# A hybrid decoder layer: every 512-column group projected in a pair, seven products for eight in 21 more chunks

## The chip, the cores and the metric

The kernel runs on one core of a Trainium2 chip. The metric is device time in microseconds (us) of one launch. Engines: TensorE (PE, matmuls), VectorE (DVE), ScalarE (ACT), GpSimd (POOL), SyncE (SP, issues DMAs).

## The reference

One layer on 256 tokens of 4096 features, in float32, cut to what matters:

```
h = rms_norm(x, norm_w)
proj = h @ w_in                        # 4096 x 13328 columns
rq, rk, rv, rg, mq, mk, mv, mg, sz, sxbc, sdt, lx, lg = split(proj)
y_ret  = rms_norm(retention(rq, rk, rv), ret_gn_w) * silu(rg)     # 4 heads of 256
y_moba = moba_attention(mq, mk, mv)    * silu(mg)                 # 8 heads of 128
y_ssm  = rms_norm(ssd(conv(sxbc), sdt) * silu(sz), ssm_norm_w)    # 16 heads of 64
y_lru  = rg_lru(conv(lx))              * silu(lg)                 # 8 blocks of 128
x = x + concat(y_ret, y_moba, y_ssm, y_lru) @ w_out               # 4096 x 4096
return rms_norm(x, final_norm_w)
```

Nearly all of the arithmetic lies in the two projections, `h @ w_in` and `y @ w_out`.

## The kernel before

**A product in float32.** Both operands are split in two halves of a rounded float32 type: the high one is a cast (ACT, L189, `whi`), the low one the rest (DVE, L190, `wlo`). A product is three matmuls, high by high, low by high, high by low, which add up in one bank of PSUM (`products`, L742 to 744, in single groups; `three`, L806 to 808, in pairs).

**Groups, chunks, half chunks.** The columns of `w_in` come in 25 groups: the first (rv, 1040 columns), then 24 of 512 columns in the order ret (4), bc (2), xs (2), mv (2), moba (4), lx (2) and the gates sz, rg, mg, lg (2 each). The 4096 rows are 16 chunks `c` of two tiles of 128 rows. Weights of a chunk of a group (512 KB) are loaded by SP in `raw` (5 buffers) and split two steps ahead of their use. Groups 0 to 16 run one by one, in the loop around L748. The last four pairs of groups run in `pair_in`: the pair has four accumulators `q` (two token halves, two groups), and a step is half a chunk, the weights of one group of the pair.

**Fast chunks.** In the chunks that `FAST_IN` names, `seven` multiplies the 2 x 2 blocks (tokens by weights of a pair) with seven products for eight, 21 matmuls for 24. Weights of the second step are combined with those of the first by four subtractions on DVE (L202, 203, 205, 207) and split in tiles `thi` and `tlo`; tokens are combined by `mix_of` in tiles `ys` ahead of time. Four more accumulators `r` take sums that belong to several outputs. They are added to the results behind the last fast chunk by `side` operations (`add`), two for each step. The output projection (`pair`, 4 pairs of 512 columns) does the same with `FAST`.

**Branch work.** What follows a projection (rotation, scores, convolution, scan, normalisation, gates) is cut in units in the queue `todo`; `slot()` takes one for each step. In a pair, units run until the first fast chunk, since the four `r` banks are those that the units use. Where instructions stand in the end is decided by a scheduler, engine by engine.

**Scaling by token.** The input is not normalised ahead of the projection: results are scaled by `rstd` when they leave PSUM (`rows_of`). Late groups use x tiles multiplied by a power of two per token (`rescale`, L277, tile `pwr`), and then `rres`.

**The end.** `row` adds x to the projected row, squares it on ACT for the norm, and multiplies by the final norm's weights into `rs`; `store_rows` scales `rs` (L945) and writes it out. x (`xres`) and these weights (`fw`) are loaded from POOL, six loads for each pair.

Of the kernel before, what the change touches and what calls it, by code (L numbers as in the profile page):

```python
# [18 lines left out]
P = 128  # L19
# [80 lines left out]
def tile_kernel(ctx: ExitStack, tc: tile.TileContext, t: dict):  # L100
# [74 lines left out]
    def split(n):  # L175
        if n >= len(chunks):
            return
        where, _, kt, nk, w = chunks[n]
        if where == "x":
            split_x(xraws.pop(n))  # L180
        raw = raws.pop(n)
        if where == "hold":
            hi, lo = pair_of(mixed[-1][0], "t", mixed[-1][1], 1024)
        else:
            hi, lo = pair_of(wp, "w", SPL + 1, WW)
        parts[n] = hi, lo

        def high_low(h, l, raw, a, b):
            A.copy(h[:, a:b], raw[:, a:b])  # L189
            V.tensor_tensor(l[:, a:b], raw[:, a:b], h[:, a:b].bitcast(F32), ALU.subtract)  # L190

        cuts = FIRST if n == 0 else CUTS if n == 1 else ((512, 1024),) if where == "fastb" else ((0, nk * w),)
        for a, b in cuts:
            high_low(hi, lo, raw, a, b)
        if where == "fasta":
            raws["a"] = raw
        elif where == "fastb":

            ra, rb = raws.pop("a"), raw
            (ha, la), (hb, lb) = (pair_of(mixed[-1][0], "t", mixed[-1][1], 1024) for _ in range(2))  # L200
# [61 lines left out]
    def stat_done():  # L262
        A.copy(ones_r, ones)
        m = sp.tile([P, 2], F32, name="m2", bufs=1)
        V.reduce_sum(m, xss, axis=AX.X)
# [20 lines left out]

    yT = [yp.tile([P, 2, S], F32, name=f"y{i}") for i in range(16)]

# [7 lines left out]
    def t1(name="t1"):  # L296
        return sp.tile([P, 512], F32, name="t1", bufs=5)

    lent = itertools.cycle([12, 14])

    def rows_of(ps, func=AF.Copy, lend=False):

        if lend:

            i = next(lent)
            tk = [yT[i + k].rearrange("p a b -> p (a b)") for k in range(2)]
        else:
# [118 lines left out]
    def moba_scores(h, q, k):  # L426
# [4 lines left out]
        V.scalar_tensor_tensor(s[:, 0:384], negd, 2.0 ** -(h + 1) / MS, ps[:, 0:384], op0=ALU.mult, op1=ALU.add)  # L431
        m = sp.tile([P, 4], F32, name="mm")
        V.reduce_max(m[:, 0:1], s[:, 0:128], axis=AX.X)
# [118 lines left out]
    def lru_split(n):  # L552
        w = st.pop(("lw", n))
        wh, wl = (sp.tile([P, 2, P], F32R, name=x) for x in ("lwh", "lwl"))
        A.copy(wh, w)
# [52 lines left out]

    def after(what, ps):
        name, i = what  # L610
        if name == "rv":
            st["v"] = [br.tile([P, 1024], F32, name="v") for _ in range(2)]
# [11 lines left out]
        elif name == "mv":  # L624
            if i == 0:
                st["v"] = [br.tile([P, 1024], F32, name="v") for _ in range(2)]
            for k in range(2):
                A.activation(st["v"][k][:, i * 512:(i + 1) * 512], ps[k], AF.Copy, scale=rstd[:, k:k + 1])
        elif name == "ret":
            tk = rows_of(ps, lend=True)  # L630
            qk = br.tile([P, 4, S], F32, name="qk")
# [5 lines left out]
        elif name == "bc":  # L637
            tk = rows_of(ps, lend=True)
            o = b4()
# [14 lines left out]
        elif name == "xs":  # L654
            tk = rows_of(ps, lend=True)

# [19 lines left out]
        elif name == "moba":  # L676
            tk = rows_of(ps, lend=True)
            qk = br.tile([P, 4, S], F32, name="qk")
# [5 lines left out]
        elif name == "lx":  # L684
            tk = rows_of(ps)

# [15 lines left out]
        else:  # L702
            todo.extend(gate(rows_of(ps, AF.Silu), Y_GATE[name] + 4 * i))
            if name == "sz" and i == 1:
# [79 lines left out]

    def mix_of(xs, c):
        pool = mixed[-1][0]
        q = pool.tile([P, 512], F32, name="ma")
# [3 lines left out]
        s = pool.tile([P, 512], F32, name="mb")  # L791
        s1, s2, s3, s4 = (s[:, i * P:(i + 1) * P] for i in range(4))
# [3 lines left out]
        V.tensor_tensor(s4, a12, s2, ALU.subtract)  # L796
        hl = pool.tile([P, 1024], F32R, name=f"ys{c}")
        A.copy(hl[:, 0:512], s)
# [42 lines left out]
    def pair_in(j, g, n):  # L841
# [10 lines left out]
        for c in range(NCH):  # L852
            for i in range(2):
# [8 lines left out]
                if c in fast:  # L862
                    if r is None:
                        assert not todo
                        r = [other[0].tile([P, 512], F32, name=other[1]) for _ in range(4)]
                    seven(xT, c, i, q, r, p, tt, c == fast[0], c == fast[-1])
                    if i == 1 and c == fast[-1]:

                        rows = [gp.tile([P, 1024], F32, name="ge") for _ in range(2)]
                        e11, e21, e12, e22 = (rows[k // 2][:, k % 2 * 512:(k % 2 + 1) * 512] for k in range(4))  # L870
                        side.append(lambda: A.copy(e11, r[0]))
# [7 lines left out]
                if r is None:  # L879
                    slot()  # L880
            if what == "sz":
                rescale(KC * c)
                rescale(KC * c + 1)
            if what == "rg":
                if c == 5:
                    while todo:
                        slot()
                    br_stack.close()
                    mixed.append((mx_stack.enter_context(tc.tile_pool(name="mx", bufs=1)), 3))
                    mixed[-1][0].tile([P, 48], F32, name="gap")  # L890
                if c in MIX_IN:
# [9 lines left out]
        else:  # L901
            for e, k in ((e11, 0), (e12, 1), (e21, 2), (e22, 3)):
                V.tensor_tensor(e, e, q[k], ALU.add)
                A.activation(e, e, AF.Silu, scale=rres[:, k // 2:k // 2 + 1])
            for i in range(2):
                todo.extend(gate([rows[i][:, 0:512], rows[i][:, 512:1024]], Y_GATE[what] + 4 * i))
        return n
# [17 lines left out]
    rs = [fp.tile([P, D], F32, name=f"rs{k}") for k in range(2)]  # L925
    mixed.append((ctx.enter_context(tc.tile_pool(name="mp", bufs=1)), 4))
# [21 lines left out]
    def extra(o):  # L948
# [3 lines left out]
        for k in range(2):  # L952
            xt = fp.tile([P, 512], F32, name="xres", bufs=4)
            nc.gpsimd.dma_start(out=xt, in_=t["x"][k * P:(k + 1) * P, o * 512:(o + 1) * 512])
            xres.append(xt)
        return fw, xres

    def pair(o, n, q, r, spare):
# [10 lines left out]
        def early():  # L969

            u = mixed[-1][0].tile([P, 512], F32, name="ma")
            w = mixed[-1][0].tile([P, 512], F32, name="mb")
            side.append(lambda: A.copy(u, p1))
# [11 lines left out]
        for c in range(NCH):  # L985
            if o == 0 and 1 <= c <= len(MIX):
                mix_of(yhl, MIX[c - 1])
            for i in range(2):
# [10 lines left out]
                else:  # L999
# [3 lines left out]
                    else:  # L1003
                        mms(yhl, q[2 + i], 1, c, p, c == 0, c == (LATE - 2 if end and i else NCH - 1))
                if c == fast[-1] and i == 1:
# [25 lines left out]

    MIX = (7, 9, 12, 2, 4)
    for j, o in enumerate(FAST):
# [52 lines left out]
```

## Time and profile before

| | us |
|---|---|
| median of three runs | 1551.89 (1551.76 to 1551.99) |
| the profiled execution | 1552.94 |
| its span, first to last instruction | 1551.2 |
| PE busy | 1534.5 |
| DVE busy | 1054.2 |
| ACT busy | 804.1 |
| POOL busy | 30.0 |

Terms of a sum come from the profiled execution, so they are taken from its own time. An engine is busy while an instruction of it runs; matmuls overlap, so PE is busy throughout even if its instructions are long.

### The profile page before, as it was taken

What the parts mean: (1) busy time and instruction counts of PE and PEld (TensorE: products, weight loads), DVE (VectorE), ACT (ScalarE), POOL (GpSimd) and SP (SyncE); (2) the same over time, 40 slices, a digit from 0 to 9 for tenths busy, and PEclk for the clock granted to TensorE, in tenths of its full rate; (3) what the DMA queues carried; (4) which work ended last, traced back from release to release, by engine and by line L of the source; (5) the groups of instructions that cost most, each with busy time, mean ns of one, the idle gap of its engine ahead of it and who ended that gap; (6) DMA issues with size and microseconds to landing.
All of it is one profiled execution on the core that took longest, in us unless ns stands there. A gap on an engine that the chain in (4) does not pass through costs nothing.

```text
span 1551.2 us, 19411 instructions
## 1 busy us (share of the span) xinstructions
PE 1534.5 (99%) x7166; PEld 1279.7 (83%) x7166; DVE 1054.2 (68%) x1431; ACT 804.1 (52%) x1077; POOL 30.0 (2%) x58
## 2 busy tenths in 40 slices
PE   9999999999999999999999999999999999999996
PEld 8988888888888788888888888888888888888885
DVE  5564444475565644545557876989879888887978
ACT  5644444454455434444448746555556555554553
POOL 0000000000000100000000000000000000000000
PEclk9999999999999999999999999999999999999998
DMA  8975555555555555545464555565655667575764
GB/s 310 310 239 189 174 174 184 181 191 191 196 187 181 202 191 192 175 174 179 169 209 170 186 191 177 166 215 202 206 189 207 214 212 237 190 238 208 238 221 165
DMA packets 89215, 311.34 MB, mean 201 GB/s; under 512 B 10352, under 2 KB 12032, under 8 KB 89120
## 3 DMA queue, kind: packets, MB, share of 16 engines
q1 hardware_dynamic: 83808, 296.70, 55.1%
q0 software_dynamic: 3440, 10.65, 2.4%
q10 hardware_dynamic: 1872, 2.76, 0.5%
q8 instruction: 56, 0.92, 0.2%
q14 instruction: 39, 0.32, 0.1%
HBM read 305.84 MB, written 4.22 MB: 200 GB/s over the span
## 4 chain that ended last, share of the span: by engine, by line
PE 92%; DMA 3%; DVE 3%; ACT 1%; issue 1%; POOL 0%; SPq 0%; ACTq 0%; POOLq 0%; DVEq 0%
PE pm L744 15%; PE pm L742 15%; PE pm L743 15%; PE pm L808 7%; PE pm L807 7%; PE pm L806 7%; PE pb L807 7%; PE pb L806 7%; PE pb L808 7%; DMA b<-in_x 1%; DVE wlo L190 1%; PE pb L319 1%; DMA b<-in_xt 1%; ACT whi L189 1%; DMA b<-csd 0%
## 5 line engine op out<-in xcount | busy, mean ns | idle before, releaser
L190 DVE TENSOR_TENSOR wlo<-raw,whi 128x1024 fp32r<-128x1024 f32 (+3 forms) x545 | 642.1, 1185 | 433.6 <-ACT whi L189 412.5
L189 ACT CAST whi<-raw 128x1024 fp32r<-128x1024 f32 (+3 forms) x545 | 552.5, 1019 | 584.0 <-PE pm L743 332.0
L742 PE MATMUL pm<-whi,xT 128*128 128x512 f32 (+1 forms) x1152 | 445.9, 387 | 1.9 <-ACT whi L189 0.9
L744 PE MATMUL pm<-wlo,xT 128*128 128x512 f32 (+1 forms) x1152 | 443.1, 385 | 1.5 <-DVE wlo L190 1.4
L743 PE MATMUL pm<-whi,xT 128*128 128x512 f32 (+1 forms) x1152 | 442.3, 384 | 0.0
L744 PEld LDWEIGHTS pm<-wlo,xT 128*128 128x128 f32 x1152 | 216.4, 188 | 46.0 <-DVE wlo L190 3.3
L742 PEld LDWEIGHTS pm<-whi,xT 128*128 128x128 f32 x1152 | 216.6, 188 | 45.0 <-ACT whi L189 1.6
L743 PEld LDWEIGHTS pm<-whi,xT 128*128 128x128 f32 x1152 | 216.6, 188 | 41.8
L806 PE MATMUL pm<-whi,xT 128*128 128x512 f32 (+1 forms) x438 | 170.1, 388 | 0.0
L808 PE MATMUL pm<-wlo,xT 128*128 128x512 f32 (+1 forms) x438 | 169.9, 388 | 0.1
L807 PE MATMUL pm<-whi,xT 128*128 128x512 f32 (+1 forms) x438 | 169.7, 387 | 0.0
L806 PE MATMUL pb<-whi,xT 128*128 128x512 f32 x398 | 155.3, 390 | 0.0
L807 PE MATMUL pb<-whi,xT 128*128 128x512 f32 x398 | 155.0, 389 | 0.0
L808 PE MATMUL pb<-wlo,xT 128*128 128x512 f32 x398 | 155.0, 389 | 0.0
L189 ACT CAST thi<-raw 128x512 fp32r<-128x512 f32 (+1 forms) x123 | 75.1, 629 | 60.0 <-DVE raw L202 36.1
L808 PEld LDWEIGHTS pm<-wlo,xT 128*128 128x128 f32 x438 | 82.3, 188 | 17.3 <-DVE wlo L190 0.6
L807 PEld LDWEIGHTS pm<-whi,xT 128*128 128x128 f32 x438 | 82.3, 188 | 16.6
L806 PEld LDWEIGHTS pm<-whi,xT 128*128 128x128 f32 x438 | 82.3, 188 | 16.5
L808 PEld LDWEIGHTS pb<-wlo,xT 128*128 128x128 f32 x398 | 74.7, 188 | 15.6
L807 PEld LDWEIGHTS pb<-whi,xT 128*128 128x128 f32 x398 | 74.7, 188 | 15.5
L806 PEld LDWEIGHTS pb<-whi,xT 128*128 128x128 f32 x398 | 74.7, 188 | 15.5
L190 DVE TENSOR_TENSOR tlo<-raw,thi 128x512 fp32r<-128x512 f32 (+1 forms) x123 | 84.4, 698 | 1.1 <-ACT thi L189 0.8
(277 smaller groups left out, 1156.5 us busy)
## 6 DMA issues: line engine op xcount, KB each, us to landing
raw<-in_w SPq DMA_DIRECT2D x384, 512.0 KB, 3.5
raw<-in_wo SPq DMA_DIRECT2D x128, 512.0 KB, 5.4
raw<-in_w SPq DMA_DIRECT2D x31, 520.0 KB, 5.0
b<-in_x SPq DMA_DIRECT2D x8, 512.0 KB, 6.1
xres<-in_x POOLq DMA_DIRECT2D x16, 256.0 KB, 5.7
b<-in_xt SPq DMA_DIRECT2D x15, 257.0 KB, 4.9
fw<-in_fnw POOLq DMA_DIRECT2D x8, 256.0 KB, 6.2
out<-rs ACTq DMA_DIRECT2D x8, 256.0 KB, 2.9
```

What stands on the lines that cost most here:

```text
L189: A.copy(h[:, a:b], raw[:, a:b])
L190: V.tensor_tensor(l[:, a:b], raw[:, a:b], h[:, a:b].bitcast(F32), ALU.subtract)
L319: T.transpose(ps[:, e * S + k * P:e * S + (k + 1) * P], tk[k][:, (2 * u + e) * P:(2 * u + e + 1) * P], ident)
L742: T.matmul(ps[:, :w], xh, hi[:, o:o + w], start=first, stop=False)
L743: T.matmul(ps[:, :w], xl, hi[:, o:o + w], start=False, stop=False)
L744: T.matmul(ps[:, :w], xh, lo[:, o:o + w], start=False, stop=last)
L806: T.matmul(ps, x[0], hi, start=first, stop=False)
L807: T.matmul(ps, x[1], hi, start=False, stop=False)
L808: T.matmul(ps, x[0], lo, start=False, stop=last)
```

## The change

1. All 24 groups of 512 columns run in pairs through `pair_in`; only rv is left to the old loop.
2. Pairs ret (second), bc, xs, moba (both) and lx have fast chunks 10, 12 and 14: 18 more. In the output projection they are 4, 6, 6 and 5 for 3, 5, 5 and 5: 3 more.
3. The scaling of the x tiles by token moves to the first pair, chunks 4 to 15, and to the first chunks of the second. From the second pair on, results are scaled by `rres`.
4. The mixed x tiles of chunks 10, 12 and 14 are made in chunks 5 to 7 of the second pair.
5. Split weight sums of the early pairs lie in tiles `yb` or `b4`, one set of four; behind the last fast chunk results are built in y tiles 12 to 15 (or `qk`).
6. In the output projection x is loaded straight into `rs`, and `row` multiplies in place. There are no `xres` buffers to wait for, so all x loads are queued at its start.
7. Small tiles get a pool of their own, and the split LRU weights one tile.

The core of the diff:

```diff
-NP = 17
-FAST_IN = {17: (), 19: (11, 13), 21: (3, 5, 7, 9, 11, 13), 23: (5, 9, 11, 13)}
-FAST = {0: (7, 9, 12), 2: (2, 4, 7, 9, 12), 4: (2, 4, 7, 9, 12), 6: (2, 4, 7, 9, 12)}
+EARLY = (10, 12, 14)
+FAST_IN = {1: (), 3: EARLY, 5: EARLY, 7: EARLY, 9: (), 11: EARLY, 13: EARLY, 15: EARLY, 17: (),
+           19: (11, 13), 21: (3, 5, 7, 9, 11, 13), 23: (5, 9, 11, 13)}
+FAST = {0: (6, 8, 10, 12), 2: (2, 4, 6, 8, 10, 12), 4: (2, 4, 6, 8, 10, 12), 6: (2, 4, 6, 8, 10)}
...
-    for gi, (what, cols) in enumerate(GROUPS[:NP]):
+    for gi, (what, cols) in enumerate(GROUPS[:1]):
...
+    def t_tiles():
+        if not mixed:
+            n = len(banks)
+            pool, tag = (yp, "yb") if n <= 5 else (br, "b4")
+            a, b, c, d = (pool.tile([P, 1024], F32R, name=tag, bufs=4) for _ in range(4))
+            return (a, b), (c, d)
+        return [pair_of(mixed[-1], "t", 3 if len(mixed) == 1 else 4, 1024) for _ in range(2)]
...
-            if what == "sz":
-                rescale(KC * c)
-                rescale(KC * c + 1)
+            if g == 1 and c >= 4:
+                rescale(KC * c - 8)
+                rescale(KC * c - 7)
+            if g == 3:
+                if c < 4:
+                    rescale(24 + KC * c)
+                    rescale(25 + KC * c)
+                elif 5 <= c < 8:
+                    k = c - 5
+                    at = gp.tile([P, 1024], F32R, name="ge") if k < 2 else sp.tile([P, 1024], F32R, name="s3", bufs=1)
+                    mix_of(xT, EARLY[k], at)
...
-        V.tensor_tensor(rs[k][:, o * 512 + a:o * 512 + b], xres[:, a:b], fw[:, a:b], ALU.mult)
+        V.tensor_tensor(xres[:, a:b], xres[:, a:b], fw[:, a:b], ALU.mult)
...
-            xt = fp.tile([P, 512], F32, name="xres", bufs=4)
+            xt = rs[k][:, o * 512:(o + 1) * 512]
```

**Where the order moves.** The first place is the bc pair, behind retention's norm. On DVE, in before, the norm's second reciprocal (of a tile `t`) and the products with it stand among low parts of weights:

```order
L190 TENSOR_TENSOR wlo<-raw,whi 128x1024 x2
L378 RECIPROCAL t_2719<-t_2719 128x512
L190 TENSOR_TENSOR wlo<-raw,whi 128x1024
L395 SCALAR_TENSOR_TENSOR y_106<-y_106,par,t_2719 128x256 x2
L395 SCALAR_TENSOR_TENSOR y_107<-y_107,par,t_2719 128x256 x2
L190 TENSOR_TENSOR wlo<-raw,whi 128x1024 x5
```

On DVE, in the changed kernel, at the same place (`raw<-raw` is a weight sum, `yb` holds the sums' halves):

```order
L194 TENSOR_TENSOR wlo<-raw,whi 128x1024 x2
L399 RECIPROCAL t_2942<-t_2942 128x512
L194 TENSOR_TENSOR wlo<-raw,whi 128x512
L416 SCALAR_TENSOR_TENSOR y_110<-y_110,par,t_2942 128x256 x2
L416 SCALAR_TENSOR_TENSOR y_111<-y_111,par,t_2942 128x256 x2
L206 TENSOR_TENSOR raw<-raw 128x512
L194 TENSOR_TENSOR wlo<-raw,whi 128x1024
L207 TENSOR_TENSOR raw<-raw 128x512
L194 TENSOR_TENSOR yb<-raw,yb 128x512
L209 TENSOR_TENSOR raw<-raw 128x512
L194 TENSOR_TENSOR yb<-raw,yb 128x512
L211 TENSOR_TENSOR raw<-raw 128x512
```

The weight sums of the first fast chunk now follow the norm directly. On PE, in before, the norm's second pair of matmuls (`ones_r`) stands in a plain row of products:

```order
L744 MATMUL pm<-wlo,xT 128x512
L375 MATMUL pb<-r_2694,ones_r 128x512
L375 MATMUL pb<-r_2695,ones_r 128x512
L742 MATMUL pm<-whi,xT 128x512
L743 MATMUL pm<-whi,xT 128x512
```

On PE, in the changed kernel, 24 matmuls behind that norm, where the second half of fast chunk 10 begins (`ge` and `yb` are the mixed tokens and the weight sums):

```order
L828 MATMUL pm<-wlo,ge 128x512
L826 MATMUL pm<-whi,xT 128x512
L827 MATMUL pm<-whi,xT 128x512
L826 MATMUL pb<-whi,xT 128x512
L827 MATMUL pb<-whi,xT 128x512
L826 MATMUL pb<-yb,ge 128x512
L827 MATMUL pb<-yb,ge 128x512
L828 MATMUL pm<-wlo,xT 128x512
```

Matmuls of the following chunk (`whi,xT`, `wlo,xT`) stand between the mixed product and those with `yb`, and among them. The second place is POOL at the start of the output projection. In before, the loads of two pairs:

```order
L950 DMA fw<-in_fnw 128x512
L954 DMA xres<-in_x 128x512 x2
L950 DMA fw<-in_fnw 128x512
L954 DMA xres<-in_x 128x512 x3
L950 DMA fw<-in_fnw 128x512
```

In the changed kernel, there:

```order
L989 DMA fw<-in_fnw 128x512
L993 DMA rs_10052<-in_x 128x512
L993 DMA rs_10053<-in_x 128x512
L989 DMA fw<-in_fnw 128x512
L993 DMA rs_10052<-in_x 128x512
L993 DMA rs_10053<-in_x 128x512
```

Twelve more loads of x into the two `rs` tiles follow, and only then the next `fw`, which waits for a buffer.

## Rows read from the trace of the kernel before

**Rows 1.** The page, busy time, share of the span and instructions of each engine.

```profile
PE 1534.5 (99%) x7166; PEld 1279.7 (83%) x7166; DVE 1054.2 (68%) x1431; ACT 804.1 (52%) x1077; POOL 30.0 (2%) x58
```

**Rows 2.** The page, chain that ended last, share of the span by engine.

```profile
PE 92%; DMA 3%; DVE 3%; ACT 1%; issue 1%; POOL 0%; SPq 0%; ACTq 0%; POOLq 0%; DVEq 0%
```

**Rows 3.** Waits of PE: line waited for, us in total, times, longest us.

```profile
PE pm L744 <- DVE wlo L190: 1.4, 2, 1.0
```

**Rows 4.** Timeline of PE, pair mg: start us, us, instruction.

```profile
1108.35 0.39 PE L806 MATMUL pm<-whi,xT 128*128 128x512 f32 x1
...
1113.79 0.39 PE L806 MATMUL pm<-whi,xT 128*128 128x512 f32 x1
```

**Rows 5.** Windows: length; PE, PEld, DVE, ACT, POOL busy; PE clock, DMA share, GB/s.

```profile
99.00:192.80 93.80, 93.12 (x422) 77.07 (x423) 49.40 (x79) 39.96 (x48) 0.52 (x1) 1.00 0.56 196
286.60:380.40 93.80, 93.80 (x426) 77.86 (x426) 57.01 (x66) 48.43 (x60) 1.06 (x2) 1.00 0.55 186
1060.00:1070.00 10.00, 10.00 (x46) 8.29 (x45) 9.44 (x13) 5.73 (x9) 0.00 (x0) 1.00 0.62 211
1203.00:1289.00 86.00, 86.00 (x384) 71.28 (x383) 72.49 (x109) 44.70 (x62) 4.21 (x8) 1.00 0.62 211
1215.00:1225.00 10.00, 10.00 (x46) 8.29 (x45) 9.78 (x21) 4.95 (x7) 0.00 (x0) 1.00 0.92 363
```

**Rows 6.** Lines by shape: busy us, mean ns of one, idle before it.

```profile
L190 DVE TENSOR_TENSOR wlo<-raw,whi 128x1024 fp32r<-128x1024 f32 x479 | 581.8, 1222 | 402.0 <-ACT whi L189 380.8 <-PE pb L319 19.4 <-PE pm L808 0.3
L190 DVE TENSOR_TENSOR tlo<-raw,thi 128x512 fp32r<-128x512 f32 x120 | 80.9, 686 | 1.1 <-ACT thi L189 0.8
L202 DVE TENSOR_TENSOR raw<-raw 128x512 f32<-128x512 f32 x30 | 20.7, 691 | 1.8 <-DMA raw<-in_wo 0.6 <-DMA raw<-in_w 0.2
L277 DVE TENSOR_TENSOR xT<-xT,pwr 128x512 fp32r<-128x512 f32 x32 | 21.8, 688 | 1.3 <-PE pm L808 1.2
L189 ACT CAST whi<-raw 128x1024 fp32r<-128x1024 f32 x479 | 499.9, 1049 | 540.9 <-PE pm L743 332.0 <-PE pm L807 95.7 <-PE pb L807 71.9
L189 ACT CAST thi<-raw 128x512 fp32r<-128x512 f32 x120 | 72.3, 619 | 58.4 <-DVE raw L202 36.1 <-DVE raw L205 18.7 <-DVE raw L203 2.3
```

**Rows 7.** Timeline of DVE, pair mg, first weight sums of two fast chunks.

```profile
1063.87 0.69 DVE L202 TENSOR_TENSOR raw<-raw 128x512 f32<-128x512 f32 x1
...
1073.90 0.69 DVE L202 TENSOR_TENSOR raw<-raw 128x512 f32<-128x512 f32 x1
```

**Rows 8.** Timelines of PE, ACT and DVE, end of the fast stretch of mg.

```profile
1093.39 0.39 PE L806 MATMUL pm<-whi,xT 128*128 128x512 f32 x1
...
1094.68 0.62 ACT L189 CAST thi<-raw 128x512 fp32r<-128x512 f32 x1 [2.47 <-DVE raw L202]
...
1101.07 0.68 DVE L190 TENSOR_TENSOR tlo<-raw,thi 128x512 fp32r<-128x512 f32 x1
...
1103.94 2.72 DVE L850 TENSOR_TENSOR ge<-ge,pb 128x512 f32<-128x512 f32 x4
```

**Rows 9.** Timelines of PE and DVE, group bc, retention's norm.

```profile
323.22 0.63 PE L375 MATMUL pb<-r,ones_r 128*128 128x512 f32 x2
...
325.79 3.35 DVE L378 RECIPROCAL t<-t 128x512 f32<-128x512 f32 x1
329.05 1.16 DVE L190 TENSOR_TENSOR wlo<-raw,whi 128x1024 fp32r<-128x1024 f32 x1
330.13 1.66 DVE L395 SCALAR_TENSOR_TENSOR y<-y,par,t 128x256 f32<-128x256 f32 x4
```

**Rows 10.** The page's DMA issues (KB each, us to landing), and POOL's timeline.

```profile
raw<-in_wo SPq DMA_DIRECT2D x128, 512.0 KB, 5.4
...
1208.89 1.07 POOL L954 DMA_DIRECT2D xres<-in_x  x2 [0.50 <-issue]
```

**Rows 11.** Timelines of PE and DVE at the end.

```profile
1538.77 0.28 PE L808 MATMUL pm<-wlo,xT 128*128 128x256 f32 x1
...
1543.01 3.39 DVE L945 TENSOR_SCALAR rs<-rs,fsm 128x256 f32<-128x256 f32 x9 [0.66 <-POOL fsm L942]
```

More of the change, by code (lines that the diff above doesn't have):

```diff
@@ L199, in split @@
             ra, rb = raws.pop("a"), raw
-            (ha, la), (hb, lb) = (pair_of(mixed[-1][0], "t", mixed[-1][1], 1024) for _ in range(2))
+            (ha, la), (hb, lb) = t_tiles()
             c1, c2 = slice(0, 512), slice(512, 1024)
@@ L284, in v_scale, with y_rest @@
                                    op1=ALU.add)
-    yT = [yp.tile([P, 2, S], F32, name=f"y{i}") for i in range(16)]
+    yT = [yp.tile([P, 2, S], F32, name=f"y{i}") if i // 4 in (0, 3) else None for i in range(16)]
+    def y_rest():
+        for i in range(4, 12, 2):
+            y = yp.tile([P, 4, S], F32, name="yb", bufs=4)
+            yT[i], yT[i + 1] = y[:, 0:2, :], y[:, 2:4, :]
     def ych(kt):
@@ L553, in lru_split @@
         w = st.pop(("lw", n))
-        wh, wl = (sp.tile([P, 2, P], F32R, name=x) for x in ("lwh", "lwl"))
+        if "lwt" not in st:
+            st["lwt"] = sp.tile([P, 1024], F32R, name="s3", bufs=1).rearrange("p (a b c) -> p a b c", a=4, b=2)
+        wh, wl = (st["lwt"][:, n % 2 * 2 + i] for i in range(2))
         A.copy(wh, w)
@@ L607, in piece, with after @@
         return st[key, e // 2][:, (e % 2) * S:(e % 2 + 1) * S]
-    def after(what, ps):
+    def after(what, ps, tk=None):
         name, i = what
+        if name not in ("rv", "mv"):
+            tk = tk or rows_of(ps, AF.Silu if name in Y_GATE else AF.Copy, name in ("ret", "bc", "xs", "moba"))
         if name == "rv":
@@ L783, in tile_kernel, with mix_of @@
     msum = {}
-    def mix_of(xs, c):
-        pool = mixed[-1][0]
-        q = pool.tile([P, 512], F32, name="ma")
+    def mix_of(xs, c, at=None):
+        pool = mixed[-1] if mixed else None
+        q = pool.tile([P, 512], F32, name="ma") if pool else t1()
         for i, y in enumerate(xs[KC * c:KC * c + 2]):
@@ L867, in pair_in @@
                     if i == 1 and c == fast[-1]:
-                        rows = [gp.tile([P, 1024], F32, name="ge") for _ in range(2)]
-                        e11, e21, e12, e22 = (rows[k // 2][:, k % 2 * 512:(k % 2 + 1) * 512] for k in range(4))
+                        if what == "lx":
+                            rows = [br.tile([P, 1024], F32, name="qk") for _ in range(2)]
+                        elif what in Y_GATE:
+                            rows = [gp.tile([P, 1024], F32, name="ge") for _ in range(2)]
+                        if rows:
+                            rows = [[w[:, 0:512], w[:, 512:1024]] for w in rows]
+                        else:
+                            rows = [[yT[k + e].rearrange("p a b -> p (a b)") for e in range(2)] for k in (12, 14)]
+                        (e11, e21), (e12, e22) = rows
                         side.append(lambda: A.copy(e11, r[0]))
@@ L888, in pair_in @@
                     br_stack.close()
[L889 to L890 removed]
+                    mixed.append(mx_stack.enter_context(tc.tile_pool(name="mx", bufs=1)))
                 if c in MIX_IN:
@@ L903, in pair_in @@
                 V.tensor_tensor(e, e, q[k], ALU.add)
-                A.activation(e, e, AF.Silu, scale=rres[:, k // 2:k // 2 + 1])
+                A.activation(e, e, AF.Silu if what in Y_GATE else AF.Copy, scale=rres[:, k // 2:k // 2 + 1])
             for i in range(2):
-                todo.extend(gate([rows[i][:, 0:512], rows[i][:, 512:1024]], Y_GATE[what] + 4 * i))
+                after(GROUPS[g + i][0], None, rows[i])
+        if g == 1:
+            rows_by.append(rres)
+        if what == "xs":
+            y_rest()
         return n
@@ L969, in early @@
         def early():
-            u = mixed[-1][0].tile([P, 512], F32, name="ma")
-            w = mixed[-1][0].tile([P, 512], F32, name="mb")
+            u = mixed[-1].tile([P, 512], F32, name="ma")
+            w = mixed[-1].tile([P, 512], F32, name="mb")
             side.append(lambda: A.copy(u, p1))
@@ L1003, in pair @@
                     else:
-                        mms(yhl, q[2 + i], 1, c, p, c == 0, c == (LATE - 2 if end and i else NCH - 1))
+                        mms(yhl, q[2 + i], 1, c, p, c == 0, c == (LATE - 1 if end and i else NCH - 1))
                 if c == fast[-1] and i == 1:
```

30 lines of the change are left out of this document (14 added, 16 removed).

## The prediction

> **What bounds the kernel now.** I read the busy times first: TensorE (PE) is busy 1534.5 of 1551.2 us, VectorE (DVE) 1054.2, ScalarE (ACT) 804.1 [rows 1]. The reader is to see that PE has no slack to speak of, and that DVE has 497 us of it. Second, the chain that ended last: 92% of it is PE, DMA and DVE 3% each [rows 2]. Third, PE's own waits: the largest entry of that view is 1.4 us, for two waits on a low part of the weights [rows 3]. So PE issues matmuls from end to end, and the time falls by the matmuls taken away, unless PE starts to wait.
>
> Last, the rate. In the pair mg, where no fast chunk lies between, the matmul at 1108.35 and the one at 1113.79 are 24 apart [rows 4]: 24 matmuls of 128x512 in 5.44 us, 0.2267 us each. (The 0.39 in those rows is the length of one; they overlap, so the spacing is the price.) The granted clock in the stretches that I looked at is 1.00 throughout, the upper level of 2.4 GHz [rows 5], so there is no cheaper matmul to be had.
>
> **The change part by part.**
>
> *Matmuls.* A fast chunk has 21 matmuls for 24. There are 18 more fast chunks ahead of the gates and 3 more in the output projection (21 for 18), so 21 x 3 = 63 matmuls go: 63 x 0.2267 = 14.28 us off PE. The orders agree: 6236 matmuls of 128x512 become 6173, every other shape keeps its count. Pairing alone changes no matmul.
>
> *Work on DVE and ACT.* Durations are those of [rows 6]. An ordinary chunk costs DVE two low parts of 1.22 us, 2.44. A fast chunk costs one of 1.22, one of half the width, 0.69, four weight sums of 0.69 and four low parts of the sums of 0.69: 7.4 us, 4.96 more. On ACT it has 1.05 + 5 x 0.62 = 4.15 for 2.10. So DVE gets 21 x 4.96 = 104 us, the additions behind six early pairs, 8 of 0.69 each, 33 us, and four more mixed x tiles at about 2.7 us (an estimate: seven smaller additions and one low part), 11 us: 148 us beside 497 idle. It is hidden if it fits stage by stage. An early pair of groups has DVE busy 57.0 of 93.8 us [rows 5]; 3 fast chunks and the additions add 3 x 4.96 + 5.5 = 20.4, and the pair shrinks by 9 x 0.2267 = 2.0: 77.4 of 91.8. The tightest stage is the first output pair with 72.5 of 86.0 [rows 5]; it gets one fast chunk and one mixed tile: 80.2 of 85.3. ACT stays near half. At nothing, then; without the cover each fast chunk would cost up to its 4.96, and that is the rivals' matter.
>
> Within a fast stretch the density is higher than the stage's mean, and here the trace has the very pattern: in the pair mg with fast chunks 3, 5, ... 13, the first weight sum of one starts at 1063.87, of the next at 1073.90 [rows 7]. That is 10.03 us for a fast and an ordinary chunk; PE needs (21 + 24) x 0.2267 = 10.2. DVE was busy 9.44 of 10 us there and PE all 10 [rows 5]. In the order of the changed kernel the new fast stretches have the same sequence on DVE, ACT and PE, but for one (the bc pair, below).
>
> One thing differs: the early pairs hold one set of four tiles for split weight sums, where mg has one and a half and the output pairs two. PE began the chunk after fast chunk 11 at 1093.39, so it had read the sums by then; the first cast into the sums of 13 began at 1094.68, and their last low part at 1101.07 [rows 8]. One set would have been free 1.29 us before it was needed. I take 0 here; a lost margin is the rival on the slower side.
>
> *The scaling of x by token* moves from the sz pair to the first pairs: 32 x 0.688 = 22 us of DVE [rows 6], into a stretch with DVE busy 49.4 of 93.8 [rows 5]. The sz pair has as much less to do. 0 us, and no DMA goes with it.
>
> *The bc pair.* Here the normalisation of retention's output lands directly ahead of the first fast chunk, 10. In before's trace its two matmuls start at 323.22, 0.23 apart; its second reciprocal runs from 325.79 to 329.14 (3.35 us), and four products of 1.66 us together follow [rows 9]. In the new order 24 matmuls stand between those two and chunk 10: 323.68 + 24 x 0.2267 = 329.1. From there PE wants the last low part of the weight sums 20 matmuls on, at 333.65. DVE, from 329.14, has in the order: low part (512), the four products, sum, low part (1024), sum, low, sum, low, sum, low, low (1024), low. With each started 0.08 us before the end of the last, as a low part of 1.16 us begun at 329.05 is followed at 330.13 [rows 9], this ends at 338.4; with full durations at 339.4. PE would be 4.75 to 5.75 us late; but the new order puts 17 matmuls of the next chunk into that stretch, 3.85 us of cover. That leaves 0.9 to 1.9 us. At chunk 12, DVE's list goes on for 8.8 to 9.9 us and ends at 347.2 to 349.3; PE, 77 matmuls after 329.1 and late by the first lag, gets there at 347.5 to 348.5: 0 to 0.8 more. Bounds 0.9 and 2.7, and I take their middle, 1.8 us, as these ends lie close. If the matmuls moved ahead are not ready either, it is up to 8 (5.75 at chunk 10 and some 2 at 12).
>
> *x loads in the output projection.* All 16 x loads (256 KB each) and two of the final norm's weights are queued on GpSimd at its start; before, they came pair by pair, the first two at 1208.89 [rows 10]. That is 18 x 0.262 = 4.7 MB beside weights that need 2 x 0.524 MB per 5.44 us = 193 GB/s. The queues moved 363 GB/s in the busiest stretch there [rows 5], so 170 GB/s are left: 28 us, about five chunks, and x is first needed behind the last fast chunk, 12 x 5.44 = 65 us on. Weight loads took 5.4 us in the median [rows 10], with five buffers to run ahead in. Cost 0. If x took half of the 363, weights would have 181 of their 193: 12 GB/s x 26 us = 0.3 MB behind, 1.6 us at 193. Bound: 2 us.
>
> A rule of the Trainium skill speaks for that bound: "DMA: Bandwidth & Descriptors", section "Queues, rings and completion order", has each DMA engine take turns, packet by packet, between the queues that have work. No run so far shows so long a queue.
>
> *The tail.* PE's last matmul ends at 1539.05; DVE's second scaling starts at 1543.01 [rows 11], 3.96 later. The last fast chunk there is 10 now and not 12, so DVE reaches the end with less behind it, while one more addition and one more product stand in front of that scaling, and a product in place must also wait for ACT's square. I take -0.5, an estimate, bounds -1 and +0.5 (about one addition and one product of 0.69 either way).
>
> **Sum** on the profiled execution: 1551.2 - 14.28 + 1.8 - 0.5 = 1538.2 us of span; 1552.94 - 1551.2 = 1.74 lie around it: 1540.0. That execution was 1.05 above the median of the runs, 1551.89. So 1538.9.
>
> **Rivals.**
> - *No lag anywhere* (the bc pair's cover holds whole): 1538.9 - 1.8 = 1537.1. For it: PE's order is rearranged just there. Against: a reciprocal of 3.35 us is more than a fast stretch leaves DVE.
> - *Gaps in more places*: 5 to 8 us in all, either the bc pair uncovered or about 0.6 to 1.0 us behind each of the eight new pairs, where up to eight additions stand in front of the next pair's banks. 1537.1 + 5 to 8: 1542.1 to 1545.1. For it: new seams of this kind. Against: the seam behind mg, additions from 1103.94 [rows 8], and no wait of PE for them.
> - *Slower: DVE becomes the bound in the early fast stretches*, since one set of sum tiles ties each fast chunk's sums to PE's end with the last. From 1093.39 PE wants the last low part of the next fast chunk 5.44 + 20 x 0.2267 = 10.0 us on; it was done at 1101.75, 8.4 us on. If DVE did three whole low parts (3 x 1.22 = 3.7 us) more in between, PE would wait 2.1 us at each of the 12 places where an early fast chunk follows another: 25 us, so 1562. It decides from 1.23 us a place (14.8 / 12: break-even), and from 1.5 the kernel is slower by over 0.2%. For it: a margin of 1.6 us. Against: the order has no such low parts there.
> - *x loads crowd the weights* at the start of the output projection: up to 2 us, 1540.9.
> - *It doesn't do what it says*: the counts of the orders speak against; 1551.9.
>
> **Chances.** Forecast 0.50 (its own range 1537.9 to 1540.5), no lag 0.20, more gaps 0.20, x loads 0.04, DVE as the bound 0.05 (of it 0.03 slower by over 0.2%, 0.02 about even), nothing done 0.01. What a measurement here can tell from no change is 0.2%, 3.1 us: faster is below 1548.8, slower above 1555.0. Faster 0.50 + 0.20 + 0.20 + 0.04 = 0.94, same 0.03, slower 0.03. The range goes from 1536.3 (no lag, and the tail at its better bound or a little below) to 1545.5 (the end of more gaps); it leaves out the last two outcomes on the slower side and the thin ends.
>
> **What would show it.** PE with 63 matmuls fewer and 14 us less busy; PE's waits with a group of some 2 us on low parts in the bc pair, at 330 to 350 us, and nothing over 1 us elsewhere; early weight sums 10.0 us apart in a fast stretch, with DVE over 9 of 10 us busy; x landing late but weight loads at 5 to 9 us; the second scaling 3.4 us behind PE's last matmul. Wrong if PE waits for sums, banks or casts in more than that pair, if it waits for a weight load near 1200 to 1230, or if DVE lags from chunk to chunk.

## The result and the profile after

The changed kernel takes 1538.64 us, median of six runs (1537.19 to 1539.60), against 1551.71 for six of the kernel before: a ratio of 0.9916, 95% interval 0.9903 to 0.9929, so it is faster by about 0.8%. The forecast was 1538.9. The profiled execution took 1537.89, with a span of 1536.1.

The page of the changed kernel, busy times and the chain that ended last, and below it the list of PE's waits (us in total, times, longest us):

```profile
PE 1520.3 (99%) x7103; PEld 1267.2 (82%) x7103; DVE 1189.5 (77%) x1675; ACT 845.1 (55%) x1170; POOL 29.6 (2%) x58
...
PE 96%; DVE 1%; DMA 1%; issue 1%; ACT 0%; POOL 0%; ACTq 0%; POOLq 0%; DVEq 0%
```

```profile
PE pm L762 <- ACT whi L193: 1.4, 1, 1.4
PE pb L826 <- ACT yb L193: 1.2, 1, 1.2
PE pb L749 <- DVE epsc L261: 1.0, 1, 1.0
PE pm L828 <- DVE wlo L194: 0.5, 2, 0.3
```

Against [rows 1] PE has 63 instructions and 14.2 us less, DVE 135 us more, and PE is still what the end hangs on [rows 2]. One wait is new, the 1.2 us on `yb`, the weight sums of an early fast chunk.

Where the span went: PE's last matmul ends 14.34 us earlier (1524.71 for 1539.05), and what follows it is 0.76 us shorter; 15.1 in all. The 63 matmuls account for 14.28 of the 14.34. The rest came out at nearly nothing, but not because nothing happened there: about 3.0 us were lost in the bc pair, and about 3.0 us of PE's small waits, which before had elsewhere, were not there. (Both are sums over PE's timeline, of what the spacing of its 512-column matmuls has over 0.2267 us, and of the waits listed.) Two of these waits in the list of the kernel before:

```profile
PE pm L742 <- ACT v L619: 0.9, 1, 0.9
...
PE pm L742 <- ACT whi L189: 0.9, 1, 0.9
```

**The bc pair.** DVE's timeline in the changed kernel, from retention's second reciprocal to the last low part of chunk 10's sums (start us, length us; compare [rows 9]):

```profile
337.76 3.34 DVE L399 RECIPROCAL t<-t 128x512 f32<-128x512 f32 x1
341.02 0.63 DVE L194 TENSOR_TENSOR wlo<-raw,whi 128x512 fp32r<-128x512 f32 x1
341.57 1.66 DVE L416 SCALAR_TENSOR_TENSOR y<-y,par,t 128x256 f32<-128x256 f32 x4
343.15 0.69 DVE L206 TENSOR_TENSOR raw<-raw 128x512 f32<-128x512 f32 x1
...
348.50 1.22 DVE L194 TENSOR_TENSOR wlo<-raw,whi 128x1024 fp32r<-128x1024 f32 x1
349.63 0.69 DVE L194 TENSOR_TENSOR yb<-raw,yb 128x512 fp32r<-128x512 f32 x1
```

PE's timeline beside it, and ACT's at the second gap:

```profile
348.11 0.40 PE L827 MATMUL pb<-yb,ge 128*128 128x512 f32 x1
348.64 0.50 PE L828 MATMUL pb<-yb,ge 128*128 128x512 f32 x1
...
355.12 0.39 PE L827 MATMUL pm<-whi,xT 128*128 128x512 f32 x1
355.54 0.51 PE L828 MATMUL pb<-yb,ge 128*128 128x512 f32 x1
357.20 0.50 PE L826 MATMUL pb<-yb,ge 128*128 128x512 f32 x1 [1.16 <-ACT yb L193]
```

```profile
355.59 1.05 ACT L193 CAST whi<-raw 128x1024 fp32r<-128x1024 f32 x1 [1.86 <-DMA raw<-in_w]
356.54 0.61 ACT L193 CAST yb<-raw 128x512 fp32r<-128x512 f32 x1
```

The last low part of chunk 10 ends 9.2 us after the reciprocal, 341.10 to 350.32, where the order with the shorter spacing gave 9.3. (In the trace chunk 10 begins 24 matmuls behind the norm's, as the prediction counted; the matmuls with `yb` that the order shows stand some 42 behind.) PE loses about 1.1 us at chunk 10, in small steps such as 0.53 us from 348.11 to 348.64, where 0.23 is the rule. At chunk 12 it loses about 1.9 more, and that has a second cause, which was not forecast: ACT's cast of a weight sum, begun at 356.54, stands in ACT's queue behind the cast of an ordinary weight chunk, and that one waits 1.86 us for its load. SP issued that load at 349.75, directly behind the low part that DVE ran from 348.50 to 349.72, near the end of the list that the norm had delayed:

```profile
349.75 0.33 SPq L164 DMA_DIRECT2D raw<-in_w  x1
```

So DVE's lag came back a second time, through the weight buffer that it freed late. This second part differs from execution to execution. Matmul by matmul against the run with retention's norm in the xs pair (below), chunk 10 loses 1.1 us in all three kept executions with this order in the bc pair (the first, the second of the changed kernel, and the run with the old output projection), and chunk 12 loses 1.9, 1.0 and 0.8. In the last of these ACT's cast does not wait for the load, so 0.8 is what chunk 12 cost without that wait.

**The other steps.** Early fast chunks in the xs pair, their first weight sums, and windows: bc pair, xs pair, one fast stretch of it, and the first output pair (length; PE, PEld, DVE, ACT, POOL busy; clock, DMA share, GB/s):

```profile
430.63 0.69 DVE L206 TENSOR_TENSOR raw<-raw 128x512 f32<-128x512 f32 x1
...
439.70 0.69 DVE L206 TENSOR_TENSOR raw<-raw 128x512 f32<-128x512 f32 x1
...
449.74 0.69 DVE L206 TENSOR_TENSOR raw<-raw 128x512 f32<-128x512 f32 x1
```

```profile
284.70:377.50 92.80, 91.31 (x410) 73.98 (x409) 67.47 (x85) 47.59 (x62) 2.15 (x4) 1.00 0.53 182
377.50:470.00 92.50, 92.50 (x423) 76.90 (x422) 72.81 (x99) 51.27 (x70) 2.12 (x4) 1.00 0.57 198
...
440.00:450.00 10.00, 10.00 (x46) 8.29 (x45) 9.48 (x13) 5.76 (x8) 0.00 (x0) 1.00 0.67 234
...
1188.00:1273.00 85.00, 85.00 (x383) 69.93 (x382) 80.19 (x129) 47.23 (x66) 9.61 (x18) 1.00 0.68 249
```

10.04 us between the last two sums and DVE at 9.48 of 10 are the pattern of [rows 5, 7]; PE is busy throughout except in the bc pair. In the output projection x took 9.9 us to land, weights 4.7 over the whole projection (issues of the page; KB each, us to landing), and PE waits for neither:

```profile
raw<-in_wo SPq DMA_DIRECT2D x128, 512.0 KB, 4.7
...
rs<-in_x POOLq DMA_DIRECT2D x16, 256.0 KB, 9.9
```

At the end the second scaling starts 3.21 us behind PE's last matmul, where it was 3.96 [rows 11]:

```profile
1524.43 0.28 PE L828 MATMUL pm<-wlo,xT 128*128 128x256 f32 x1
...
1527.92 3.38 DVE L984 TENSOR_SCALAR rs<-rs,fsm 128x256 f32<-128x256 f32 x9 [0.66 <-POOL fsm L981]
```

### The profile page after: what moved, and what is told of

Same layout as the page of the kernel before. It is cut to its first block, busy times and chain, and to the rows that moved or that the text cites. A ratio compares the mean times of both kernels' runs of the same rounds, so it can differ in the third digit from the quotient of the medians.

```text
span 1536.1 us, 19726 instructions
## 1 busy us (share of the span) xinstructions
PE 1520.3 (99%) x7103; PEld 1267.2 (82%) x7103; DVE 1189.5 (77%) x1675; ACT 845.1 (55%) x1170; POOL 29.6 (2%) x58
## 4 chain that ended last, share of the span: by engine, by line
PE 96%; DVE 1%; DMA 1%; issue 1%; ACT 0%; POOL 0%; ACTq 0%; POOLq 0%; DVEq 0%
PE pm L828 15%; PE pm L826 15%; PE pm L827 15%; PE pb L826 14%; PE pb L828 14%; PE pb L827 14%; PE pm L764 1%; PE pm L762 1%; PE pm L763 1%; PE pb L340 1%; PE pm L340 1%; PE pb L763 1%; PE pb L764 1%; PE pb L762 0%; DMA b<-in_xt 0%
## 5 line engine op out<-in xcount | busy, mean ns | idle before, releaser
L826 PE MATMUL pm<-whi,xT 128*128 128x512 f32 (+1 forms) x907 | 355.0, 391 | 0.0
L828 PE MATMUL pm<-wlo,xT 128*128 128x512 f32 (+1 forms) x907 | 352.2, 389 | 0.5 <-DVE wlo L194 0.5
L827 PE MATMUL pm<-whi,xT 128*128 128x512 f32 (+1 forms) x907 | 352.3, 388 | 0.0
L826 PE MATMUL pb<-whi,xT 128*128 128x512 f32 x827 | 324.3, 392 | 0.0
L828 PE MATMUL pb<-wlo,xT 128*128 128x512 f32 x827 | 322.1, 389 | 0.0
L827 PE MATMUL pb<-whi,xT 128*128 128x512 f32 x827 | 321.9, 389 | 0.0
L828 PEld LDWEIGHTS pm<-wlo,xT 128*128 128x128 f32 x907 | 170.3, 188 | 36.7 <-DVE wlo L194 1.4
L826 PEld LDWEIGHTS pm<-whi,xT 128*128 128x128 f32 x907 | 170.4, 188 | 34.8 <-issue 0.4
L827 PEld LDWEIGHTS pm<-whi,xT 128*128 128x128 f32 x907 | 170.4, 188 | 34.1
L828 PEld LDWEIGHTS pb<-wlo,xT 128*128 128x128 f32 x827 | 155.3, 188 | 32.5
L826 PEld LDWEIGHTS pb<-whi,xT 128*128 128x128 f32 x827 | 155.3, 188 | 31.9 <-ACT whi L193 0.2
L827 PEld LDWEIGHTS pb<-whi,xT 128*128 128x128 f32 x827 | 155.4, 188 | 31.6
L762 PE MATMUL pm<-whi,xT 128*128 128x256 f32 (+1 forms) x128 | 43.0, 337 | 1.6 <-ACT whi L193 1.4
L763 PE MATMUL pm<-whi,xT 128*128 128x256 f32 (+1 forms) x128 | 42.9, 337 | 0.0
L193 ACT CAST b<-raw 128x512 fp32r<-128x512 f32 x36 | 22.1, 620 | 31.6 <-DVE raw L206 17.8
L206 DVE TENSOR_TENSOR raw<-raw 128x512 f32<-128x512 f32 x51 | 35.3, 692 | 1.9 <-DMA raw<-in_w 0.2
L207 DVE TENSOR_TENSOR raw<-raw 128x512 f32<-128x512 f32 x51 | 35.3, 692 | 1.5
```

Of the source, the lines that this page charges most:

```text
L762: T.matmul(ps[:, :w], xh, hi[:, o:o + w], start=first, stop=False)
L763: T.matmul(ps[:, :w], xl, hi[:, o:o + w], start=False, stop=False)
L826: T.matmul(ps, x[0], hi, start=first, stop=False)
L827: T.matmul(ps, x[1], hi, start=False, stop=False)
L828: T.matmul(ps, x[0], lo, start=False, stop=last)
```

## The experiments

Each group of runs has runs of the kernel before beside it on the same chip, and ratios are to those; a median of before was 1553.43, 1552.86 and 1552.78 us in the three groups. A time in an expectation stands on the 1551.7 of the first runs, so it is judged by its distance to the changed kernel. The changed kernel itself stands only in the first group (with the runs of the bc pair and of retention's norm); the others are set against it by their ratios. "Lag" is PE's excess in the bc pair over that of a pair like it (0.7 to 0.8 us).

**The changed kernel again.**

> The changed kernel again, as the measure for the three runs beside it. Its six runs so far go from 1537.2 to 1539.6 us, median 1538.6. Theory: PE idles about 2.7 us in the bc pair (about 0.9 us at fast chunk 10, 1.8 us at fast chunk 12), because retention's norm (two reciprocals of 3.35 us) keeps DVE from the weight sums. Expected 1538.6, with that idle time in the bc pair again. Rival: the idle time there differs from execution to execution, and makes the spread of the runs.

1540.75 us (1538.26 to 1543.48), ratio 0.9917 [0.9902, 0.9933]. The lag was 2.4 us in the profiled execution, 3.0 in the first; that does not make a spread of 5 us, so the rival has little of it. This execution has a wait at the seam behind rv that the first had not. PE waits there for rv's copies out of PSUM (on ACT `v`, on DVE `v` and `dt`), which free the banks that the first pair writes. Behind it the granted clock fell to its lower level, 0.50, where the first execution has 1.00 in the same window (length; PE, PEld, DVE, ACT, POOL busy; clock, DMA share, GB/s):

```profile
PE pm L826 <- ACT v L644: 2.0, 1, 2.0
```

```profile
102.00:104.00 2.00, 2.00 (x6) 1.51 (x6) 2.00 (x5) 0.00 (x0) 0.00 (x0) 0.50 0.99 371
```

Eight matmuls of 128x512 stand 0.43 us apart there, for 0.23: 1.6 us more, beside the wait of 2.0. The spread of the runs goes the same way: of the 37 runs of the kernel before in the three groups, the 13 above 1554 us all have a mean granted clock of 0.996, and 23 of the 24 below it have 0.997 or 0.998. Where the clock fell in runs without a trace is not shown.

**The bc pair without fast chunks.**

```diff
-FAST_IN = {1: (), 3: EARLY, 5: EARLY, 7: EARLY, ...
+FAST_IN = {1: (), 3: EARLY, 5: (), 7: EARLY, ...
```

> The bc pair has no fast chunks; all else is as in the changed kernel. 9 matmuls come back: 9 x 0.2267 = 2.04 us. Theory (the norm ahead of the fast chunks makes the lag of about 2.7 us): the lag goes with them, 1538.6 + 2.0 - 2.7 = 1537.9, so this pair's three fast chunks earn nothing. Rival (the lag comes from the norm alone, or from pairing, with fast chunks or without): the lag stays, 1540.7.

1539.91 us, ratio 0.9912 [0.9899, 0.9926]: 0.8 under the changed kernel beside it, where the theory had 0.7 under and the rival 2.0 over. The intervals overlap; the trace decides: the lag is 0. So neither the norm nor the pairing makes it without fast chunks.

**Fast chunks 12 and 14 only.**

```diff
+FAST_IN = {1: (), 3: EARLY, 5: (12, 14), 7: EARLY, ...
```

> The bc pair has fast chunks 12 and 14 only, so the first weight sums are wanted two chunks (10.9 us) later after the norm. 3 matmuls come back, 0.7 us. Theory (DVE is late only because the sums follow the norm directly): the lag goes, 1538.6 + 0.7 - 2.7 = 1536.6. Rival (a fast chunk in this pair is late wherever it stands, since weight buffers come free late): a lag of 1.5 us or more stays at chunk 12, 1538 or more.

1535.79 us, ratio 0.9887 [0.9874, 0.9901]. The lag is 0, the rival's lag at chunk 12 is not there. The time is 5.0 under the changed kernel, 2.0 expected. The rest is not this pair's: in the profiled executions PE's time through every later pair is the same to 0.3 us, but PE is 2.7 us ahead already behind rv. Of that, 0.9 is a shorter wait behind rv (1.1 us for 2.0) and 1.6 the clock, which is 1.00 there.

**Retention's norm in the xs pair.**

```diff
-            if i == 3:
-                todo.append(None)
-                norm_units(Y_RET, "gnw")
...
+            if i == 0:
+                norm_units(Y_RET, "gnw")
             todo.append(None)
             todo.append(lambda: (turn(tk, 0, "bcT"), turn(tk, 1, "bcT")))
```

> All 21 more fast chunks stay; retention's norm is queued at the start of the xs pair and not behind retention's last unit in the bc pair, so nothing long stands ahead of the bc pair's weight sums. Theory: the lag of about 2.7 us goes and nothing comes back, 1538.6 - 2.7 = 1535.9. Rival (the norm costs the same wherever it stands, since the xs pair has fast chunks too): 1538.6, with PE idle in the xs pair.

1538.58 us (1535.88 to 1541.84), ratio 0.9901 [0.9884, 0.9918], 2.2 under the changed kernel. All 21 fast chunks are there and the lag is 0; the reciprocals now run at 384 and 392 us and PE does not wait for them, so the rival is out. The window in which the changed kernel had 91.31 us of PE has all of its 92.80 here (the pair lies some 4.7 us later in this execution, and PE does not idle up to its end either):

```profile
284.70:377.50 92.80, 92.80 (x428) 77.33 (x427) 61.43 (x77) 48.44 (x64) 2.15 (x4) 1.00 0.58 192
```

So the norm directly ahead of the weight sums is what makes the lag. The gain is small and unsure in time: in this execution the wait for rv's copies was 3.0 us, and the granted clock behind it was 0.50 again from 102 to 104 us.

**Other banks for the first pair.**

```diff
-        pools = [(pm, "pm"), (pb, "pb")][::-1 if j % 2 else 1]
+        pools = [(pm, "pm"), (pb, "pb")][::1 if j % 2 else -1]
```

> As the run with retention's norm queued in the xs pair, and every pair starts in the other four PSUM banks, so that the first pair after rv begins in two banks that rv did not use. Theory: PE's wait of 0 to 3.0 us for rv's copies (behind a cast on ACT whose weight load lands late, from 95.9 to 99.0 us) falls to under 0.7 us, since those banks are wanted half a chunk (2.7 us) later. Mean of the waits seen is 1.6: some 1.3 us faster than that run, about 15 us faster than before (ratio 0.990), and a narrower spread. Rival (PE then waits for the late weight load itself): the same wait half a chunk on, no gain.

1537.01 us, ratio 0.9901 [0.9887, 0.9916]: no gain that the ratio shows. In its profiled execution the wait at the seam is 0.9 us and on DVE's copy of `dt`, the other half of rv's epilogue. What stands ahead of that copy in DVE's queue is the low part of a weight chunk, which waits for ACT's cast, which waits for a load:

```profile
98.47 1.05 ACT L193 CAST whi<-raw 128x1024 fp32r<-128x1024 f32 x1 [5.05 <-DMA raw<-in_w]
```

```profile
99.56 1.23 DVE L194 TENSOR_TENSOR wlo<-raw,whi 128x1024 fp32r<-128x1024 f32 x1 [4.87 <-ACT whi L193]
```

So a late weight load holds rv's copies up on both engines, and other banks do not change that. Why the load is late this run does not show; the run without the small write, below, does.

**Pairs without the early fast chunks.**

```diff
+FAST_IN = {1: (), 3: (), 5: (), 7: (), 9: (), 11: (), 13: (), 15: (), 17: (),
```

> All pairs as in the changed kernel, but without the 18 early fast chunks. 54 matmuls come back: 12.24 us. Theory (price of the fast chunks is PE's alone and all DVE and ACT work of theirs is hidden, but for the lag of 2.4 to 3.0 us in the bc pair): 12.24 - 2.7 = 9.5 us slower than the changed kernel, 3.4 us faster than before (2.04 from the output projection, the rest from the tail and small waits). Rival (the work of the fast chunks costs elsewhere too): less than 8 us slower than the changed kernel.

1551.24 us, ratio 0.9989 [0.9979, 0.9998]: 1.7 under before and some 11 over the changed kernel, between 9.5 of the theory and 12.24, the bare price of 54 matmuls. The lag is 0, so up to 3 us of those 12.24 should have come back; but this execution had 3.7 us of excess in its first 100 us, the changed kernel 1.3 and 2.2. The 1.7 under before is also only half of the 3.4 expected. The rival is out by the ratio and by the trace: the 18 fast chunks cost nothing outside the bc pair that would show.

**Low parts of the early weight sums twice, and half of them.**

```diff
             V.tensor_tensor(l[:, a:b], raw[:, a:b], h[:, a:b].bitcast(F32), ALU.subtract)
+            if where == "fastb" and not mixed and b - a == 512 and h is not hi:   # and a == 0, for half
+                V.tensor_tensor(l[:, a:b], raw[:, a:b], h[:, a:b].bitcast(F32), ALU.subtract)
```

> In the 18 early fast chunks the four low parts of the weight sums are computed twice: 4 x 0.6 to 0.69 = 2.4 to 2.8 us more on DVE per fast chunk, 43 to 50 us in all. Theory (DVE has a margin of 1.6 us per early fast chunk before PE waits): about 1.0 us at each of the 12 places where an early fast chunk follows another, and 3 to 6 us more in the bc pair that has no margin: 15 to 18 us slower than the changed kernel. Rival A (DVE stays off the path): the same time but for the bc pair, 3 to 6 us slower. Rival B (no margin at all): 40 us slower or more.

> As the run with four low parts twice, but two of them: 1.2 to 1.4 us more on DVE per early fast chunk. Theory (margin of 1.6 us): hidden in five of the six pairs; in the bc pair 1.3 us for each of two or three fast chunks: 3 to 4 us slower than the changed kernel, all of it in the bc pair. Rival B (no margin): 20 us slower.

Four more: 1551.72 us, ratio 0.9990 [0.9980, 1.0001], 11 over the changed kernel; two more: 1543.67, ratio 0.9942 [0.9925, 0.9959], 3 to 4 over it. Between the same matmuls of the first profiled execution of the changed kernel, PE lost in the ret, xs, first moba, second moba and lx pairs 1.8, 1.8, 1.8, 0.9 and 0.9 us more with four more low parts, and 0.4, 0.4, 0.4, 0.1 and 0.1 with two. In the bc pair it lost 4.4 and 0.4 more; of the 4.4, 1.6 are the granted clock, which was 0.50 from 360 to 362 us behind two waits of 0.84 us for the sums. The execution with two more is also 2.0 us late by the end of rv, and that is not the sums'. The waits of the kernel with four more name the sums, which the changed kernel's list has once:

```profile
PE pb L830 <- DVE yb L196: 3.0, 4, 0.8
```

With 1.2 to 1.4 us more per fast chunk nearly all is hidden; with 2.4 to 2.8 more, 0.9 us shows at each of the two places of the ret, xs and first moba pairs. So the margin there is 1.5 to 1.9 us (2.4 to 2.8 less 0.9, an estimate), as [rows 8] had it with 1.6, and more in the last two pairs. The mechanism of the slower rival exists, then, but the changed kernel does not reach it. With four more its size was under the theory's (11 for 15 to 18); with two more it was near it (3 to 4), but not all in the bc pair as expected.

**No small write in front of the weights.**

```diff
-        nc.gpsimd.dma_start(out=pwd.rearrange("o (a p) -> p (o a)", a=2), in_=pw)
-        nc.gpsimd.dma_start(out=pwr, in_=pwd.to_broadcast([P, S]))
+        dg = sp.tile([P, 512], F32R, name="r1", bufs=3)
+        for k in range(2):
+            V.tensor_scalar(dg[:, k * P:(k + 1) * P], ident, pw[:, k:k + 1], None, op0=ALU.mult)
+        ps = bank()
+        T.matmul(ps[:, 0:S], ones_r, dg[:, 0:S], start=True, stop=True)
+        V.tensor_copy(pwr, ps[:, 0:S])
```

> As the run with retention's norm queued in the xs pair; and the powers of two per token come to all partitions by a matmul of ones with two diagonal blocks (128x256), not by a 1 KB write to memory (9.5 us) and a read back. In the changed kernel DMA moves 20 to 100 GB/s from about 85 to 94 us, while that write is under way, and the weight loads behind it land late (median 8.4 to 11.6 us); ACT's cast of one waits, rv's copies wait behind the cast, and PE waits 0 to 3.0 us for them. Theory (the small write holds the weight loads up): DMA does not stall there, the wait is gone, and with the bc lag gone too the time is 1535.5 where before is 1551.7 (ratio 0.9895), with a spread under 2 us. Rival (the loads stall for another reason: their buffers come free late at the seam): the stall near 85 to 95 us and the wait of PE stay, ratio 0.990 or more.

1536.67 us (1535.30 to 1537.16), ratio 0.9892 [0.9879, 0.9906]: the theory's ratio, and the spread of 1.9 us is under the 2 that it named. All four runs are below all ten of the changed kernel, which were taken in other groups. It has all of its fast chunks and, by the trace, none of its two larger waits; that the run with two fast chunks in the bc pair has a lower ratio, 0.9887, lies within both intervals. What DMA moves from 70 to 101 us, 40 slices of 0.78 us, first in the changed kernel, then in this one:

```profile
GB/s 258 300 376 392 252 300 371 434 375 352 376 394 406 289 169 333 355 365 266 25 85 0 0 26 58 37 37 26 21 16 53 280 418 418 412 375 206 407 418 423
```

```profile
GB/s 309 247 273 393 404 268 348 371 398 370 362 366 287 380 356 173 287 352 351 341 40 95 407 222 196 344 143 164 344 174 159 322 122 132 259 264 74 254 365 42
```

The hole of 9 us, from slice 20 to 31, is gone, and with it the wait behind rv; the granted clock does not fall behind rv either. The hole begins with the write of 1 KB, issued on POOL at 83.25 for which the read back waits 8.94 us; 512 KB weight loads issued from 70 to 101 us took 8.4 us in the median, against 3.9 here. In the changed kernel's second execution ACT stood in a cast for such a load while rv's copies and PE waited behind it:

```profile
83.25 0.89 POOL L285 DMA_DIRECT2D pwd<-pw  x1 [0.51 <-DVE rres L283]
93.08 0.58 POOL L286 DMA_DIRECT2D pwr<-pwd  x1 [8.94 <-DMA pwd<-pw]
```

```profile
98.75 1.04 ACT L193 CAST whi<-raw 128x1024 fp32r<-128x1024 f32 x1 [5.15 <-DMA raw<-in_w]
99.70 0.85 ACT L644 COPY v<-pm 128x512 f32<-128x512 f32 x2
```

The kernel before has the same write, and with it a like hole: 21 to 63 GB/s in the eight slices from 90 to 96 us. So what this run gains over the changed kernel at the seam is not owed to the change, and the kernel before could have it too:

```profile
86.31 0.89 POOL L272 DMA_DIRECT2D pwd<-pw  x1 [0.51 <-DVE rres L270]
```

**The output projection's fast chunks as before.**

```diff
-FAST = {0: (6, 8, 10, 12), 2: (2, 4, 6, 8, 10, 12), 4: (2, 4, 6, 8, 10, 12), 6: (2, 4, 6, 8, 10)}
+FAST = {0: (7, 9, 12), 2: (2, 4, 7, 9, 12), 4: (2, 4, 7, 9, 12), 6: (2, 4, 7, 9, 12)}
...
```

> The changed kernel with the output projection's fast chunks as before (3, 5, 5, 5, the last at 12). 9 matmuls come back, 2.04 us. Theory: the tail is longer again too, since DVE is full with chunk 12's sums at the end: second scaling 3.9 us behind PE's last matmul and not 3.2; 2.0 + 0.7 = 2.7 us slower than the changed kernel. Rival (the tail's gain comes from x in the row buffer and not from the fast chunks): 3.2 us stays, 2.0 us slower.

Two more lines of the kernel, which follow from these lists, change with them. It took 1543.99 us, ratio 0.9940 [0.9924, 0.9955], some 3.6 over the changed kernel by the ratios, which cannot tell 2.7 from 2.0. The trace can: the second scaling starts 4.15 us behind PE's last matmul, where it is 3.2 in every other kept execution of the new output projection. So the tail's gain comes from the fast chunk that left the end. x in the row buffer by itself saves nothing there.

```profile
1527.15 0.28 PE L828 MATMUL pm<-wlo,xT 128*128 128x256 f32 x1
...
1531.58 3.38 DVE L984 TENSOR_SCALAR rs<-rs,fsm 128x256 f32<-128x256 f32 x9 [0.66 <-POOL fsm L981]
```

## Why the prediction was right, point by point

- **Matmuls, -14.28.** Right: 63 instructions, 14.2 us of PE's busy time. The run without the early fast chunks and the one with the old output projection give back their parts. The price per matmul held in the first execution, at a granted clock of 1.00 from 102 to 104 us; in the second it did not for eight matmuls behind rv, which the prediction had no term for.
- **DVE and ACT work, nothing.** Right. DVE's busy time rose by 135 us, forecast 148; the first output pair has 80.2 of 85, as forecast; the bc pair 67.5 of 92.8, where an early pair was forecast at 77. The margin per early fast chunk, 1.6 us by the rows, is 1.5 to 1.9 in three pairs by the runs with more low parts, and more in two.
- **One set of sum tiles, scaling of x, x loads: nothing.** Right by the list of waits: none of PE's is on a token scale, or on a load near 1190 to 1230. Nor did a cast wait for a tile of sums that was still being read: ACT's idle time before its casts into these tiles was ended by DVE's sums (17.4 of 19.3 us before those into `yb`, 30.2 of 31.6 before those into `b4`). The x loads did queue (9.9 us to land), and weight loads had up to 8.5 us there, inside what five buffers cover, for PE did not wait. The rule cited from the Trainium skill ("DMA: Bandwidth & Descriptors", "Queues, rings and completion order") is neither borne out nor refuted by that: the queues together moved up to 425 GB/s there, more than the 363 that the bound was worked out from.
- **The bc pair, +1.8.** The place and the first cause were right; three experiments that take the norm or the sums away make the lag 0. The size was 3.0 and 2.4 us, and 2.1 in the run with the old output projection. The first half of the term, 0.9 to 1.9 at chunk 10, held with 1.1. The failing part is the second half: 0 to 0.8 at chunk 12 was counted on DVE's list alone, and it measured 1.9, 1.0 and 0.8. The late DVE also kept a weight buffer, so a load came late, and ACT, which takes its casts in order, passed that on to a weight sum; the 0.8 of the execution without that wait is the forecast's own upper bound.
- **The tail, -0.5.** It was -0.76.
- **Not in the sum:** about 3 us of waits of the kernel before, mostly in its first 100 us and behind rv, which were shorter in the first profiled execution. They are not the change's doing: the second profiled execution of the changed kernel had them back, with 2.0 us behind rv and the lower clock there. That the median hit the forecast within 0.3 us is luck, since that and the undersized lag cancel; the steps are good to about 1.5 us each, not to 0.3. One sign that the prediction named failed: PE was to wait for nothing over 1 us outside the bc pair, and it waited 1.4 us for a cast in rv (0.9 in before) and, in the second execution, 2.0 behind rv.

## What to carry to other kernels

When PE never waits, price a change by its matmuls and then look, row by row in the new order, for long instructions of other engines right ahead of the new work; moving one reciprocal pair to another stage was worth some 9 to 14 matmuls by the traces. Follow a lag one step further than the engine that is late: to the buffers that it frees, the loads that wait for them, and what stands behind those loads' readers in a queue that is worked off in order. Look at the kernel's small DMAs too: one of 1 KB held the weight loads up for 9 us here. And where PE does wait, read the granted clock behind the wait as well: behind rv a wait of 2.0 us came with 1.6 us more of slow matmuls.

## What the runs showed of the hardware

A write of 1 KB to memory, ordered as 256 pieces of one float, took 8.7 to 10.4 us to land in the eleven traces that have it, and for most of that time the weight loads on another queue and all else together moved under 100 GB/s, of the 170 to 430 that there were before and after. Why is open; that it goes with this write and its read back is shown by taking both away, which removed the hole and the wait of up to 3.0 us on PE.

The granted clock fell to its lower level (0.50, 1.2 GHz) right behind PE's wait of 2.0 us at the seam in the second execution of the changed kernel, behind the wait of 3.0 us there with retention's norm in the xs pair, and in the run with four more low parts behind the seam's wait of 2.0 us, behind two of 0.84 us in the bc pair, and once in its first 15 us. Each of the falls at the seam and in the bc pair made some eight 128x512 matmuls stand 0.43 us apart for 0.23, 1.6 us in all; then the clock was back at 1.00.
